# Operand sums, leftover products and fetches reordered in the two half-steps of a diffusion trunk

## The chip, the cores and the metric

The kernel runs on one core of one Trainium2 chip. The metric is the device time of one execution in microseconds. The profile counts from the first to the last instruction of one profiled execution (its span); all times of single instructions come from that execution. PE is TensorE, DVE is VectorE, ACT is ScalarE, POOL is GpSimd, SP is SyncE, which issues transfers.

## The reference, cut to what matters

One layer of a trunk with 640 tokens (512 latent, 128 context) of width 1024, all in float32:

```python
def swiglu(h, w1, w3, w2):
    return (jax.nn.silu(h @ w1) * (h @ w3)) @ w2

def layer(x, mods, l, p, ctx):
    hh = rmsnorm(x, g[0]) * (1 + m[1]) + m[0]
    x = x + 0.5 * m[2] * swiglu(hh, p['ffn1_w1'][l], p['ffn1_w3'][l], p['ffn1_w2'][l])
    hh = rmsnorm(x, g[1]) * (1 + m[4]) + m[3]
    y, ctx_out = token_mixer(hh, p, l, ctx)
    x = x + m[5] * y
    hh = rmsnorm(x, g[2]) * (1 + m[7]) + m[6]
    x = x + 0.5 * m[8] * swiglu(hh, p['ffn2_w1'][l], p['ffn2_w3'][l], p['ffn2_w2'][l])
```

The change lies in the two half-steps, the `swiglu` terms before and after the token mixing. Their inner width is 2816. `m` are the nine modulation vectors, a product of the conditioning with a large matrix.

## The kernel before, in words

**Numbers.** Every float32 matrix operand is held as two parts, high and low (value minus high). A product takes three matmuls per block of 128: high with high, high with low, low with high. ScalarE makes the high part by a copy, VectorE the low part by a subtraction.

**Seven products instead of eight.** The tokens are two halves of 320 columns, the contraction is two halves, and the weights' output columns are two halves. A granule of weights (128 partitions x 2048, 1 MB) is multiplied in Winograd's form of Strassen's scheme: seven products A11, S1, S2, A12, S3, S4, A22 with sums of operand quarters, where the plain form has eight. One product on a granule is 12 matmuls of 128 x 320 (four blocks, three each). They go into three accumulators X, Y, Z; results are finished by additions.

- `operand_sums` makes the four sums S1, S2, S3, S4 of the quarters of the normalised input, each in two halves r: `terms` (a VectorE subtraction or addition in place, in the memory of x, then ScalarE's copy of the high part) and `low` (VectorE). Their VectorE instructions are chained by hand. S4 lies in a quarter of `hm`, S1 to S3 in tiles `S`.
- `Granule.parts` makes from the raw weights the high and low parts of three quarters (`wB`, `wC`) and then forms three sums in place in `raw` (three VectorE instructions). `Granule.sums` splits `raw` as a whole into `ww` high (L286, ScalarE) and low (VectorE). S1, S2, S3 and A22 read `ww`.
- `products` runs over the granules. For granule i TensorE does A11, S1, then A22 of granule i - 1 (`tail[0]`), S2, then S4 of granule i - 1 (`tail[1]`), A12 and S3: so two products of each granule are left over to the next. Beside them stand the load of granule i + 2 into one of two `raw` buffers, `parts` and `sums` of granule i + 1, the copies `u2`, `u3` of accumulators (ScalarE) and the additions that finish results (`done`).

**Stages of a half-step.** Block 0 (256 of the 2816 columns) is done plainly. Then come 20 granules of the up product, w1 and w3 in turn for blocks 1 to 10; the gated results go by `store_g` to `g_dram`. Then the down product reads them back as operands (`fetch`). In the first half-step (`run_whole`) the down product is plain, in three block groups of four granules j each; its weights are split by `Whole.split` (L304), and columns of the modulation are computed beside it on VectorE (L712, from rows `csil` that are read back from `csil_dram`), tied behind `self.at_vec`. In the second half-step (`run`) the down product is plain for the first three blocks and in seven products for two groups of four blocks; there the operand tiles `at[q]` of a later group are fetched into tiles that earlier products have left.

**What sets the order.** TensorE's instructions are kept as written. On the other engines a planner draws the order when the program is built, by a timeline of its own; `tc.issue_after(ins)` adds that the instructions issued under it, on the engine of `ins`, come behind `ins`. Each engine takes its instructions strictly in the drawn order, and so do the queues: `nc.sync` issues on SP, `nc.gpsimd` on POOL. Before the change, in the second half-step, the parts of granule i + 1 are issued behind `copied` (ScalarE's copy of X into Y) and behind `gr.low` (VectorE's part of `sums` of granule i).

Of the kernel before, what the change touches and what calls it, by code (L numbers as in the profile page):

```python
# [31 lines left out]
def tile_trunk(ctx: ExitStack, tc: tile.TileContext, a: dict):  # L32
# [210 lines left out]
    class Granule:  # L243
# [5 lines left out]
        def load(self):  # L249
            self.raw = rawp.tile([128, 2048], F32, tag="raw", name="raw")[:, : 512 * self.nk].rearrange("p (k n) -> p k n", n=256)  # L250
            return self.fetch(self.raw)

# [3 lines left out]
        def parts(self, fp, ties=()):  # L256
            ties = iter(ties)

            def tied(*args):
                with ExitStack() as st:  # L260
                    t = next(ties, None)
                    if t is not None:
                        st.enter_context(tc.issue_after(t.ins))
                    tt(vec, *args)

# [16 lines left out]
        def sums(self):  # L282
            nk = self.nk
            t = self.two(wp, "w", 2048, None)
            flat = self.raw.rearrange("p k n -> p (k n)")
            act(t[0], flat, AF.Copy)  # L286
            self.low = tt(vec, t[1], flat, t[0].bitcast(F32), ALU.subtract)
            for i, o in ((S1, 0), (S3, 128), (A22, 256 * nk), (S2, 256 * nk + 128)):
                self.w[i] = [[w[:, o + 256 * k : o + 256 * k + 128] for k in range(nk)] for w in t]

    class Whole(Granule):


        def split(self, fp=None):
# [8 lines left out]
            for (c0, c1, h), (_, _, lw) in zip(*t):  # L303
                act(h, flat[:, c0:c1], AF.Copy)  # L304
                tt(vec, lw, flat[:, c0:c1], h.bitcast(F32), ALU.subtract)
            self.t = t
# [7 lines left out]
    class HalfStep:  # L314
# [34 lines left out]
        def operand_sums(self, pair):  # L349
# [30 lines left out]
            for f, i, r in (  # L380
                (terms, S1, 0), (terms, S1, 1), (terms, S3, 0), (low, S1, 0), (terms, S2, 0), (low, S1, 1), (terms, S3, 1),
                (terms, S2, 1), (low, S2, 0), (low, S2, 1), (low, S3, 0), (low, S3, 1), (terms, S4, 0), (terms, S4, 1),
            ):
                f(i, r)
                if (f, i) == (low, S2):
                    behind = prev.ins
            low(S4, 0)
            low(S4, 1)
            return behind

# [34 lines left out]
        def products(self, work, between, then=(), behind=None, prepared=False, first=()):  # L425
# [11 lines left out]
            for i, (gr, A, done, used) in enumerate(work):  # L437
# [25 lines left out]
                if self.n_plain < FB and i:  # L463
                    next_parts(copied, gr.low)
                into(Z, S1, True)
                if last:
                    p5 = copy_of(Z, *(("nrv",) if then else ("nt", 2)))
                if tail:
                    tail[0]()
# [4 lines left out]
                into(Y, S2, False)  # L474
                u2 = copy_of(Y, "nacc" if i < 2 * FB - 2 else "nsq", 2)
                if tail:
                    tail[1]()
                into(X, A12, False)
                done(0, 0, X, None)
                between(i, 1)  # L480
                into(Y, S3, False)
                u3 = copy_of(Y, "nry")
                if last:
# [60 lines left out]
        def run_whole(self, x, gate, final, between, behind, first):  # L544
# [6 lines left out]

            def fetch(q, i):
                b0, b1 = PLAIN_GROUPS[q]
                nc.gpsimd.dma_start(out=at[q][i][:, :, : b1 - b0].bitcast(F32), in_=self.g_dram[i, :, :, b0:b1, :])

            order = {A11: (0, 0), S1: (0, 1), S2: (0, 2), A12: (0, 3), S4: (1, 0), A22: (1, 1), S3: (1, 2)}
            work[-1][3] = lambda i: fetch(*order[i])
            self.products(work, between, down[:2], behind=behind, first=first)
# [18 lines left out]
            for q in G:  # L577
                last = q == G[-1]
                for j in range(4):
                    m = 4 * q + j  # L580
                    if m + 2 < len(down):
                        down[m + 2].load()
                    if m + 1 < len(down):
                        down[m + 1].split(self.fp if last and j < 2 else None)
                    for hf in range(1 if last and j else 2):
                        between(len(work) + m, hf)
                        for f in range(2):
                            unit(q, j, f, hf)
# [6 lines left out]

        def run(self, x, gate, final, behind=None, first_ties=()):

# [17 lines left out]

            def between(i, at):
                if (i, at) == (0, 1):
                    with tc.issue_after(work[1][0].low.ins):
# [6 lines left out]
            def down_done(q, j):  # L625
# [8 lines left out]
                def used(i):  # L634
                    if (q, j, i) == (1, 1, S3):
                        fetch(2, A11, nc.gpsimd)
                        fetch(2, S1, nc.gpsimd)
                    elif q == 1 and j == 3 and i in moves:
# [90 lines left out]
    with ExitStack() as ph:  # L729
# [133 lines left out]
        hs.gate_plain(1, 1, ps)  # L863
        hs.operand_sums(lambda r: x_all[:, 2 * r : 2 * r + 2, :])
        x_stack.close()
# [1159 lines left out]
    for f in range(2):  # L2025
        hs.gate_plain(f, 1, (ps[f, 0], ps[f, 1]))
    summed = hs.operand_sums(lambda r: x_pairs[r])
    for g in range(4):
        nc.sync.dma_start(out=x_pairs[g], in_=x2_dram[:, 2 * g : 2 * g + 2, :])
    hs.run(  # L2030
        lambda: x, half_m[:, 1], lambda d, hf: nc.sync.dma_start(out=a["y"][:, d, half(hf)], in_=x[d][:, half(hf)]),
        behind=summed, first_ties=[normed_last] * 5,
    )
# [128 lines left out]
```

## Time and profile before

| | |
|---|---|
| median of 3 runs | 1828.14 us (1828.11 to 1829.18) |
| profiled execution | 1830.94 us, span 1829.2 us |
| granted TensorE clock, mean | 0.993 |
| TensorE (PE) busy | 1788.6 us, 98% |
| VectorE (DVE) busy | 1293.0 us, 71% |
| ScalarE (ACT) busy | 830.3 us, 45% |
| chain that ended last | PE 88%, DVE 5%, DMA 4%, ACT 2% |

A row of the timeline gives the start in the span, the duration, the engine, the source line, the operation with output and inputs, the count of instructions merged into the row, and in brackets how long the engine was idle before and what released it. The line is that of a helper: L39 is any two-operand VectorE instruction, L52 any matmul, so the tiles' names tell instructions apart. A row of the waits gives who waited for whom, the sum in us, the count, and the longest. A row of windows gives the stretch, its length, busy time and count of PE, weight loads, DVE, ACT and POOL, the granted clock, the busy share of the transfer engines and GB/s. A row of a transfer queue gives packets, MB and share of the 16 engines: q0 is POOL's queue, q1 is SP's. A row of a transfer gives the count, KB of each, and the median time from issue to landing.

### The profile page before, as it was taken

How to read it: one execution, taken by the hardware profiler on the slowest of the kernel's cores; microseconds unless marked ns; L12 is line 12 of the kernel's file. 1: busy time of each engine (PE TensorE's matmuls, PEld its weight loads, DVE VectorE, ACT ScalarE, POOL GpSimd, SP SyncE). 2: the span in 40 equal slices, each digit the busy share in tenths (PEclk: the TensorE clock that was granted, in tenths of full speed). 3: DMA queues.
4: the chain of work that ended last, by engine and by line, in shares of the span. 5: the costliest groups of instructions: out<-in, count | busy, mean ns of one | idle time of the engine just before them, and what ended most of it. 6: DMA issues, size and time to landing. Idle time of an engine off the chain costs nothing.

```text
span 1829.2 us, 30479 instructions
## 1 busy us (share of the span) xinstructions
PE 1788.6 (98%) x12498; PEld 1757.0 (96%) x12498; DVE 1293.0 (71%) x2188; ACT 830.3 (45%) x1439; POOL 51.6 (3%) x93
## 2 busy tenths in 40 slices
PE   6999999999999999999999999999999899999989
PEld 4999999999999999999999999899999899999989
DVE  6888886485776668665665458787768778886576
ACT  6644544112654453444544465562326445553232
POOL 0000001010000000000000000000000000000000
PEclk9999999999999999999999999999999999999999
DMA  8344438963334234232232355676542445557952
GB/s 336 121 173 155 159 136 315 350 223 109 127 110 139 85 121 146 75 119 77 75 111 92 104 169 158 212 248 213 198 179 72 156 150 188 175 182 275 343 211 83
DMA packets 127244, 304.98 MB, mean 167 GB/s; under 512 B 9985, under 2 KB 89217, under 8 KB 114433
## 3 DMA queue, kind: packets, MB, share of 16 engines
q1 hardware_dynamic: 116242, 257.09, 40.9%
q0 software_dynamic: 10864, 45.95, 7.4%
q8 instruction: 98, 1.61, 0.4%
q14 instruction: 40, 0.33, 0.1%
HBM read 234.20 MB, written 63.63 MB: 163 GB/s over the span
## 4 chain that ended last, share of the span: by engine, by line
PE 88%; DVE 5%; DMA 4%; ACT 2%; issue 1%; SPq 0%; DVEq 0%; ACTq 0%
PE ps_f L52 44%; PE ps_p L52 22%; PE ps_t L52 11%; PE sc L52 2%; PE ps_o L52 2%; PE ps_n L52 2%; DMA ada<-csil_dram 2%; PE ps_u L52 1%; PE ps_wT L55 1%; DVE junk L712 1%; DVE wL L39 1%; DMA raw_a<-in_w_ada_c 1%; DMA raw_a<-in_w_ada_k 1%; DMA x<-in_x 1%; DMA zT_dram<-so 0%
## 5 line engine op out<-in xcount | busy, mean ns | idle before, releaser
L52 PE MATMUL ps_f<-S,ww 128*128 128x320 f32 x1992 | 319.9, 310 | 5.6 <-ACT ww L286 3.8
L52 PEld LDWEIGHTS ps_f<-S,ww 128*128 128x128 f32 x1992 | 300.6, 189 | 6.1 <-ACT ww L286 4.1
L52 PE MATMUL ps_p<-hH,wH 128*128 128x320 f32 x864 | 273.4, 316 | 0.0
L52 PE MATMUL ps_p<-hH,wL 128*128 128x320 f32 x864 | 267.0, 309 | 0.0
L52 PE MATMUL ps_p<-hL,wH 128*128 128x320 f32 x864 | 266.8, 309 | 0.0
L52 PE MATMUL ps_f<-hm,ww 128*128 128x320 f32 x1248 | 200.5, 313 | 7.7 <-ACT ww L286 4.1
L52 PEld LDWEIGHTS ps_f<-hm,ww 128*128 128x128 f32 x1248 | 189.9, 191 | 8.7 <-ACT ww L286 4.4
L52 PE MATMUL ps_t<-wH,hH 128*128 128x256 f32 x640 | 184.5, 288 | 2.2 <-DVE qT L39 1.7
L52 PE MATMUL ps_t<-wH,hL 128*128 128x256 f32 x640 | 181.3, 283 | 1.1 <-DVE hL L39 1.1
L52 PE MATMUL ps_t<-wL,hH 128*128 128x256 f32 x640 | 180.9, 283 | 0.0
L39 DVE TENSOR_TENSOR ww<-raw,ww 128x2048 fp32r<-128x2048 f32 (+1 forms) x62 | 138.8, 2238 | 41.3 <-ACT ww L286 27.0
L52 PEld LDWEIGHTS ps_p<-hL,wH 128*128 128x128 f32 x864 | 162.5, 188 | 0.5
L52 PEld LDWEIGHTS ps_p<-hH,wH 128*128 128x128 f32 x864 | 162.4, 188 | 0.5
L52 PEld LDWEIGHTS ps_p<-hH,wL 128*128 128x128 f32 x864 | 162.2, 188 | 0.0
L52 PE MATMUL ps_f<-hm,wB 128*128 128x320 f32 x1008 | 161.5, 309 | 0.0
L52 PEld LDWEIGHTS ps_f<-hm,wB 128*128 128x128 f32 x1008 | 151.3, 188 | 0.0
L39 DVE TENSOR_TENSOR wL<-raw,wH 128x2048 fp32r<-128x2048 f32 x49 | 112.1, 2289 | 40.4 <-ACT wH L122 40.3
L122 ACT ACTIVATE wH<-raw 128x2048 fp32r<-128x2048 f32 x49 | 93.7, 1912 | 75.1 <-PE ps_p L52 70.4
L52 PEld LDWEIGHTS ps_t<-wH,hH 128*128 128x128 f32 x640 | 122.6, 192 | 3.1 <-PE ps_t L52 2.3
L39 DVE TENSOR_TENSOR raw<-raw 128x1024 f32<-128x1024 f32 x144 | 124.5, 865 | 1.4
L52 PEld LDWEIGHTS ps_t<-wH,hL 128*128 128x128 f32 x640 | 122.5, 191 | 1.5 <-DVE hL L39 1.5
L52 PEld LDWEIGHTS ps_t<-wL,hH 128*128 128x128 f32 x640 | 122.6, 192 | 0.2
(295 smaller groups left out, 3156.9 us busy)
## 6 DMA issues: line engine op xcount, KB each, us to landing
g_dram<-g SPq DMA_DIRECT2D x44, 640.0 KB, 4.2
raw_a<-in_w_ada_c SPq DMA_DIRECT2D x32, 512.0 KB, 3.9
raw<-in_w1b SPq DMA_DIRECT2D x11, 1024.0 KB, 4.8
raw<-in_w3b SPq DMA_DIRECT2D x11, 1024.0 KB, 6.7
raw<-in_w1a SPq DMA_DIRECT2D x10, 1024.0 KB, 4.9
raw<-in_w3a SPq DMA_DIRECT2D x10, 1024.0 KB, 4.8
hm<-g_dram POOLq DMA_DIRECT2D x8, 1280.0 KB, 10.1
raw_a<-in_w_ada_k SPq DMA_DIRECT2D x8, 1024.0 KB, 11.2
```

Source lines behind the costliest of these rows:

```text
L39: return eng.tensor_tensor(out=out, in0=in0, in1=in1, op=op)
L52: tc.keep_in_program_order(nc.tensor.matmul(*args, **kw))
L55: tc.keep_in_program_order(nc.tensor.transpose(*args, **kw))
L122: act(h, raw, AF.Copy)
L712: vec.tensor_tensor_reduce(out=junk, in0=raw, in1=self.csil[:, v, :], op0=ALU.mult, op1=ALU.add, scale=1.0, scalar=0.0, accum_out=mod[:, c ...
```

## The change

Four things are done.

- `operand_sums` no longer makes S4 at its end; it returns a function `last` that does, and the point `behind` which the next parts follow is now the end of S3's low parts. In the second half-step `rest` calls it from `between(0, 0)`, tied behind the last VectorE instruction of granule 1's parts, and issues the four reloads of x behind it. In the first half-step it is called at once, as before.
- In the up product of the second half-step, for granules 1 and 2, the leftover product A22 goes ahead of S1 instead of behind it.
- There, and in the second half-step's down products, the additions and copies of `tail[1]`, of A12 and `u3` are tied behind the next granule's last in-place sum (VectorE) and behind its high part of `ww` (ScalarE); and a granule's parts are tied behind the high part of the `sums` before.
- Fetches: in the first half-step the three tiles S4, A22 and S3 of block group 1 are fetched on SP behind the weight loads of the first three granules of the down product, instead of on POOL at the end of the up product; and the modulation is tied behind the low part of the weights' split. In the second half-step the first two tiles of group 2 are fetched on SP behind the load of group 1's last granule, instead of on POOL.

```diff
@@ -248,7 +248,8 @@

         def load(self):
             self.raw = rawp.tile([128, 2048], F32, tag="raw", name="raw")[:, : 512 * self.nk].rearrange("p (k n) -> p k n", n=256)
-            return self.fetch(self.raw)
+            self.loaded = self.fetch(self.raw)
+            return self.loaded

         def two(self, pool, tag, n, bufs):
             return [pool.tile([128, n], F32R, tag=tag + c, name="w" + tag, bufs=bufs)[:, : n // 4 * self.nk] for c in "HL"]
@@ -261,7 +262,7 @@
                     t = next(ties, None)
                     if t is not None:
                         st.enter_context(tc.issue_after(t.ins))
-                    tt(vec, *args)
+                    self.at_vec = tt(vec, *args)

             nk, raw = self.nk, self.raw
             lo, hi = raw[:, :, 0:128], raw[:, :, 128:256]
@@ -283,7 +284,7 @@
             nk = self.nk
             t = self.two(wp, "w", 2048, None)
             flat = self.raw.rearrange("p k n -> p (k n)")
-            act(t[0], flat, AF.Copy)
+            self.high = act(t[0], flat, AF.Copy)
             self.low = tt(vec, t[1], flat, t[0].bitcast(F32), ALU.subtract)
             for i, o in ((S1, 0), (S3, 128), (A22, 256 * nk), (S2, 256 * nk + 128)):
                 self.w[i] = [[w[:, o + 256 * k : o + 256 * k + 128] for k in range(nk)] for w in t]
@@ -302,7 +303,7 @@
                 t = [((0, 1024, B[i]), (1024, n, C[i])) for i in range(2)]
             for (c0, c1, h), (_, _, lw) in zip(*t):
                 act(h, flat[:, c0:c1], AF.Copy)
-                tt(vec, lw, flat[:, c0:c1], h.bitcast(F32), ALU.subtract)
+                self.low = tt(vec, lw, flat[:, c0:c1], h.bitcast(F32), ALU.subtract)
             self.t = t

         def w(self, i, k, f):
@@ -379,14 +380,19 @@

             for f, i, r in (
                 (terms, S1, 0), (terms, S1, 1), (terms, S3, 0), (low, S1, 0), (terms, S2, 0), (low, S1, 1), (terms, S3, 1),
-                (terms, S2, 1), (low, S2, 0), (low, S2, 1), (low, S3, 0), (low, S3, 1), (terms, S4, 0), (terms, S4, 1),
+                (terms, S2, 1), (low, S2, 0), (low, S2, 1), (low, S3, 0), (low, S3, 1),
             ):
                 f(i, r)
-                if (f, i) == (low, S2):
-                    behind = prev.ins
-            low(S4, 0)
-            low(S4, 1)
-            return behind
+            behind = prev.ins
+
+            def last(ins=None):
+                nonlocal prev
+                prev = ins or prev
+                for f in (terms, low):
+                    for r in range(2):
+                        f(S4, r)
+
+            return behind, last

         def store_g(self, SO, b):

@@ -461,11 +467,14 @@
                 into(X, A11, True)
                 copied = act(Y, X, AF.Copy)
                 if self.n_plain < FB and i:
-                    next_parts(copied, gr.low)
+                    next_parts(copied, gr.low, gr.high)
+                early = tail and self.n_plain < FB and i in (1, 2) and not prepared
+                if early:
+                    tail[0]()
                 into(Z, S1, True)
                 if last:
                     p5 = copy_of(Z, *(("nrv",) if then else ("nt", 2)))
-                if tail:
+                if tail and not early:
                     tail[0]()
                 if not last:
                     work[i + 1][0].sums()
@@ -473,13 +482,23 @@
                     then[0].split()
                 into(Y, S2, False)
                 u2 = copy_of(Y, "nacc" if i < 2 * FB - 2 else "nsq", 2)
+                def behind_parts():
+                    st = ExitStack()
+                    if self.n_plain < FB and (i in (1, 2) or prepared) and not last:
+                        for t in (work[i + 1][0].at_vec, work[i + 1][0].high):
+                            st.enter_context(tc.issue_after(t.ins))
+                    return st
+
                 if tail:
-                    tail[1]()
+                    with behind_parts():
+                        tail[1]()
                 into(X, A12, False)
-                done(0, 0, X, None)
+                with behind_parts():
+                    done(0, 0, X, None)
                 between(i, 1)
                 into(Y, S3, False)
-                u3 = copy_of(Y, "nry")
+                with behind_parts():
+                    u3 = copy_of(Y, "nry")
                 if last:
                     done(1, 1, p5, u3)
                     into(Z, S4, False)
@@ -549,12 +568,12 @@
             G = range(len(PLAIN_GROUPS))
             at = [[self.ops[i] for i in (A11, S1, S2, A12)], [self.ops[i] for i in (S4, A22, S3)], [self.ops[i] for i in (S1, S2)]]

-            def fetch(q, i):
+            def fetch(q, i, eng=nc.gpsimd):
                 b0, b1 = PLAIN_GROUPS[q]
-                nc.gpsimd.dma_start(out=at[q][i][:, :, : b1 - b0].bitcast(F32), in_=self.g_dram[i, :, :, b0:b1, :])
+                eng.dma_start(out=at[q][i][:, :, : b1 - b0].bitcast(F32), in_=self.g_dram[i, :, :, b0:b1, :])

             order = {A11: (0, 0), S1: (0, 1), S2: (0, 2), A12: (0, 3), S4: (1, 0), A22: (1, 1), S3: (1, 2)}
-            work[-1][3] = lambda i: fetch(*order[i])
+            work[-1][3] = lambda i: order[i][0] == 0 and fetch(*order[i])
             self.products(work, between, down[:2], behind=behind, first=first)
             for q, tag, nb in ((1, "gA", 4), (2, "SO", 4), (2, "gB", 3)):
                 at[q].append(self.fp.tile([128, 2, nb, HALF], F32R, tag=tag, name="op"))
@@ -579,9 +598,13 @@
                 for j in range(4):
                     m = 4 * q + j
                     if m + 2 < len(down):
-                        down[m + 2].load()
+                        loaded = down[m + 2].load()
+                    if m < 3:
+                        with tc.issue_after(loaded):
+                            fetch(1, m, nc.sync)
                     if m + 1 < len(down):
                         down[m + 1].split(self.fp if last and j < 2 else None)
+                        self.at_vec = down[m + 1].low
                     for hf in range(1 if last and j else 2):
                         between(len(work) + m, hf)
                         for f in range(2):
@@ -593,7 +616,7 @@
                 for f in range(2):
                     unit(G[-1], j, f, 1)

-        def run(self, x, gate, final, behind=None, first_ties=()):
+        def run(self, x, gate, final, behind=None, first_ties=(), rest=None):


             def nothing(*args):
@@ -614,6 +637,8 @@
             first = self.SO

             def between(i, at):
+                if (i, at) == (0, 0):
+                    rest(work[1][0].at_vec)
                 if (i, at) == (0, 1):
                     with tc.issue_after(work[1][0].low.ins):
                         self.store_g(first, 0)
@@ -633,8 +658,9 @@

                 def used(i):
                     if (q, j, i) == (1, 1, S3):
-                        fetch(2, A11, nc.gpsimd)
-                        fetch(2, S1, nc.gpsimd)
+                        with tc.issue_after(last[3][0].loaded):
+                            fetch(2, A11)
+                            fetch(2, S1)
                     elif q == 1 and j == 3 and i in moves:
                         fetch(2, moves[i], nc.gpsimd)

@@ -861,7 +887,7 @@
             for k in range(KT):
                 hs.plain(ps[i], W[i], 1, 1, k)
         hs.gate_plain(1, 1, ps)
-        hs.operand_sums(lambda r: x_all[:, 2 * r : 2 * r + 2, :])
+        hs.operand_sums(lambda r: x_all[:, 2 * r : 2 * r + 2, :])[1]()
         x_stack.close()
         hs.store_g(hs.SO, 0)

@@ -2024,12 +2050,16 @@
                 hs.plain(ps[f, i], W[i], f, 1, k)
     for f in range(2):
         hs.gate_plain(f, 1, (ps[f, 0], ps[f, 1]))
-    summed = hs.operand_sums(lambda r: x_pairs[r])
-    for g in range(4):
-        nc.sync.dma_start(out=x_pairs[g], in_=x2_dram[:, 2 * g : 2 * g + 2, :])
+    summed, fourth = hs.operand_sums(lambda r: x_pairs[r])
+
+    def rest(ins):
+        fourth(ins)
+        for g in range(4):
+            nc.sync.dma_start(out=x_pairs[g], in_=x2_dram[:, 2 * g : 2 * g + 2, :])
+
     hs.run(
         lambda: x, half_m[:, 1], lambda d, hf: nc.sync.dma_start(out=a["y"][:, d, half(hf)], in_=x[d][:, half(hf)]),
-        behind=summed, first_ties=[normed_last] * 5,
+        behind=summed, first_ties=[normed_last] * 5, rest=rest,
     )


```

## The prediction

> **What bounds the kernel now.** I read the page first, then TensorE's waits, then the timeline around the long ones, then windows with the granted clock, then the transfers.
>
> ```profile
> span 1829.2 us, 30479 instructions
> PE 1788.6 (98%) x12498; PEld 1757.0 (96%) x12498; DVE 1293.0 (71%) x2188; ACT 830.3 (45%) x1439; POOL 51.6 (3%) x93
> PE ps_f L52 <- ACT ww L286: 8.0, 2, 4.1
> PE ps_f L52 <- DVE ww L39: 5.4, 3, 2.2
> ```
>
> TensorE is the bound; only time in which it waits or runs slowly can be won. The `ps_f` rows are 13.4 us, nearly all of it at three places in the half-steps. In the second half-step, `L286` is `sums` of a granule. Its first place, in time order (each product is 12 matmuls):
>
> ```profile
> 1428.72 1.92 PE L52 MATMUL ps_f<-S,ww 128*128 128x320 f32 x12
> 1430.48 1.92 PE L52 MATMUL ps_f<-hm,wB 128*128 128x320 f32 x12
> 1438.58 3.04 PE L52 MATMUL ps_f<-S,ww 128*128 128x320 f32 x10 [1.77 <-DVE ww L39]
> 1444.55 1.92 PE L52 MATMUL ps_f<-S,ww 128*128 128x320 f32 x12
> ```
>
> The pitch of a product is 1430.48 - 1428.72 = 1.76 us, 0.147 a matmul. The product A11 of granule 1 starts at 1430.48; S1, A22 of granule 0 and S2 follow. S2 should start at 1430.48 + 3 x 1.76 = 1435.76 and starts at 1444.55: **8.79 us lost**. The second place (granules of block group 1 of the down product) and the third (first half-step, down product):
>
> ```profile
> 1740.32 1.92 PE L52 MATMUL ps_f<-S,wB 128*128 128x320 f32 x12
> 1755.12 1.92 PE L52 MATMUL ps_f<-S,wC 128*128 128x320 f32 x12
> 340.43 2.21 PE L52 MATMUL ps_f<-hm,ww 128*128 128x320 f32 x14
> 344.81 2.58 PE L52 MATMUL ps_f<-hm,ww 128*128 128x320 f32 x10 [2.16 <-DVE ww L39]
> 349.68 1.92 PE L52 MATMUL ps_f<-hm,ww 128*128 128x320 f32 x12
> 346.00:348.00 2.00, 2.00 (x10) 2.00 (x9) 2.00 (x6) 0.00 (x0) 0.36 (x1) 0.50 0.72 259
> ```
>
> From 1740.32 to 1755.12 run four products, 7.04 us; 14.80 passed: **7.76 lost**. From 340.43 to 349.68 run three, 5.28; 9.25 passed: **3.97 lost** at a wait of 2.16. The last row, a window, says why a wait costs more than itself: behind it the granted clock (third column from the end) is 0.50, where undisturbed windows (such as 1425 to 1430, below) have 1.00. Together 8.79 + 7.76 + 3.97 = 20.5 us can be won.
>
> [...] The third place went to 0.50 after 2.16, so I price leftover waits by that row, 1.8 us on top.
>
> **The change, first place.** Who held `ww` of granule 1:
>
> ```profile
> 1425.04 1.55 DVE L39 TENSOR_TENSOR x<-x 128x640 f32<-128x640 f32 x2
> 1426.51 1.22 DVE L39 TENSOR_TENSOR wB<-raw,wB 128x1024 fp32r<-128x1024 f32 x1
> 1427.65 0.69 DVE L39 TENSOR_TENSOR wC<-raw,wC 128x512 fp32r<-128x512 f32 x1
> 1428.25 1.56 DVE L39 TENSOR_TENSOR hm<-x,hm 128x640 fp32r<-128x640 f32 x2
> 1429.72 1.22 DVE L39 TENSOR_TENSOR raw<-raw 128x1024 f32<-128x1024 f32 x1
> 1431.56 1.41 DVE L39 TENSOR_TENSOR raw<-raw 128x512 f32<-128x512 f32 x2
> 1432.84 1.05 ACT L271 ACTIVATE wB<-raw 128x1024 fp32r<-128x1024 f32 x1
> 1434.30 1.90 ACT L286 ACTIVATE ww<-raw 128x2048 fp32r<-128x2048 f32 x1
> 1436.23 2.29 DVE L39 TENSOR_TENSOR ww<-raw,ww 128x2048 fp32r<-128x2048 f32 x1 [3.26 <-ACT ww L286]
> ```
>
> The fourth operand sum is four VectorE instructions (two `x<-x`, two `hm<-x,hm`), mixed into the five of the next granule's parts. Moved behind them, the parts run from 1425.04: 1.14 + 0.60 (pitches) + 1.22 + 1.41 = 1429.41. The new tie to `gr.high` puts the later granule's ScalarE parts (1432.84 to 1434.30) behind this `ww`; the copy runs 1429.41 + 1.90 = 1431.31, VectorE's low part ends at 1431.33 + 2.29 = 1433.62, against 1438.52 now. The leftover product A22 goes ahead of S1, so S1 starts at 1430.48 + 3.52 = 1434.00 and needs the low part with its third matmul, 1434.29: covered by 0.67 us. What is late next: A22 needs ScalarE's copy `u3`, ready at 1430.68 but queued on ScalarE behind `ww` and perhaps behind the two copies of the moved sum:
>
> ```profile
> 1427.50 0.73 ACT L373 ACTIVATE hm<-x 128x640 fp32r<-128x640 f32 x1
> 1430.68 0.44 ACT L422 ACTIVATE u<-ps_f 128x320 f32<-128x320 f32 x1 [1.32 <-PE ps_f L52]
> ```
>
> Directly behind `ww` it ends at 1431.75, before A22's 1432.24; behind both copies at 1431.31 + 1.46 + 0.44 = 1433.21, 0.97 late. I take the middle, 0.5. The other end: both copies and both low parts of the moved sum get ahead of `ww`; then its low part ends at 1433.62 + 1.46 + 1.47 = 1436.55, a wait of 2.26, with the clock 4.1 left over. Below nothing is excluded: product order is fixed, and TensorE does no less.
>
> The moved sum itself: its product S4 comes at 1434.00 + 3.52 = 1437.52, its low parts follow `ww` on VectorE and end at 1433.62 + 1.47 = 1435.1: nothing. Granule 2: parts from about 1436.9 (an addition 0.4 and the store's subtraction 1.4 come first), then 4.37, 1.90 and 2.29 end at 1445.5; its S1, again one product later, needs it at 1446.6. Covered by 1.1. The same rows give the early A22 nothing where `ww` is on time: it only swaps two products.
>
> The four reloads of x go with the sum to about 1435.1 on SP, ahead of or behind the load of granule 3:
>
> ```profile
> x<-x_dram SPq DMA_DIRECT2D x4, 640.0 KB, 5.3
> raw<-in_w3b SPq DMA_DIRECT2D x9, 1024.0 KB, 6.9
> 1425.00:1430.00 5.00, 5.00 (x36) 5.00 (x35) 5.00 (x8) 2.24 (x4) 0.00 (x0) 1.00 1.00 326
> ```
>
> That load could issue at 1433.6 after the change, when granule 1's buffer is free. Behind all of x (4 x 640 KB = 2.62 MB, 8.0 us at 326 GB/s) and its own 1.05 MB (3.2) it lands at 1446.3; ScalarE wants it at 1445.5, and 1.05, 4.37, 1.90 and 2.29 from there end at 1455.9, against 1457.2 needed (granule 3's S1 is not early: 12.32 - 1.76 behind granule 2's). Nothing, with 1.3 to spare.
>
> **Second place.** Two group-2 fetches go from POOL to SP, behind the last load of group 1:
>
> ```profile
> 1718.35 0.70 POOL L610 DMA_DIRECT2D S<-g_dram  x1 [3.25 <-PE ps_f L52]
> hm<-g_dram POOLq DMA_DIRECT2D x4, 1280.0 KB, 7.5
> 1720.39 0.97 SPq L74 DMA_DIRECT2D raw<-in_w2b  x2
> q0 software_dynamic: 133, 0.68, 82.4%
> q1 hardware_dynamic: 133, 0.14, 19.1%
> 1735.24 0.44 ACT L422 ACTIVATE u<-ps_f 128x320 f32<-128x320 f32 x1 [4.86 <-PE ps_f L52]
> 1735.58 1.05 ACT L271 ACTIVATE wB<-raw 128x1024 fp32r<-128x1024 f32 x1
> ```
>
> The weights of granule 2 are issued at 1720.39 into fetches of 1280 KB each, of which the first of the two is the row of 1718.35. From 1726 to 1728 both queues get 133 packets, but POOL's (q0) carry 0.68 MB and the weights' (q1) 0.14. ScalarE starts the parts at 1735.58, so the weights were there by then. Two fetches less (2.62 MB at 0.34 MB/us) is 7.7 us less beside them: there by 1727.9, ahead of granule 1's A11 (1740.32 - 7 x 1.76 = 1728.00), behind which and one copy ScalarE takes them, at 1730.4. Then 1.05, VectorE's 4.37 with one residual between (put at 0.7, half the 1.41 row), 1.90 and 2.29 end at 1740.7; S1 needs it at 1742.08 + 0.29 = 1742.37. Covered by 1.7, since the additions tied behind the parts no longer hold them. The bound: ScalarE keeps the parts behind `u` (1735.24). Then 1735.68 + 1.05 + 4.37 + 1.90 + 2.29 = 1745.3, a wait of 2.9, with the clock 4.7 left over. The two fetches are read at group 2's start, three granules of 12.32 us behind 1728.00. The copy `u3` and the evictions tied behind the parts release nothing that TensorE reaches before the next granule's S1, which needs those parts itself: nothing.
>
> **Third place.** Three of the seven fetches at the end of the up product go from POOL to SP, behind the weights.
>
> ```profile
> raw<-in_w2a SPq DMA_DIRECT2D x2, 512.0 KB, 27.1
> q0 software_dynamic: 349, 1.71, 82.0%
> q1 hardware_dynamic: 346, 0.39, 21.4%
> 308.80 28.68 DMA ada<-csil_dram
> 342.47 2.28 DVE L39 TENSOR_TENSOR ww<-raw,ww 128x2048 fp32r<-128x2048 f32 x1
> ```
>
> The weights took 27.1 us, `csil` 28.68 beside POOL's fetches (315 to 320: 349 packets against 346). VectorE then ran three modulation products and split `ww` at 342.47, just as TensorE wanted it. With three fetches (3.9 MB) less on POOL at about 0.34 MB/us both land some 12 us sooner, near 323 and 326. The split's buffer is free when TensorE leaves the granule before last, 340.43 - 7 x 1.76 = 328.1; a copy of about 1.9 and VectorE's 2.28 end at 332, ten before the need: 3.97 won. The new at_vec keeps modulation behind the split: nothing. On SP the first waits until TensorE has left S4; a weight load then stands behind at most one fetch, 1.31 MB or some 4 us at the 0.34, and each granule of the down product lasts 8 x 1.76 = 14 us; group 1 is read only four granules on.
>
> **The sum:** 20.5 - 0.5 = 20.0 us. The profiled execution took 1830.94, its span 1829.2; the span should be 1809.2, that execution 1810.9. The median shown, 1828.14, is 2.80 below it; from it I forecast 1808.1.
>
> **Rivals.** (1) The moved sum gets ahead of `ww`: 4.1 left at the first place, 1828.1 - 16.4 = 1811.7. For it: the order on ScalarE today shows parts ahead of `ww`. Against: the low parts need copies that come after it. Chance 0.14. (2) ScalarE keeps granule 2 behind `u`: 1828.1 - 20.0 + 4.7 = 1812.8; 0.08. (3) Queues change nothing: bytes are the same, so the weights land as late; the third place stays and the second keeps 4.7: 1808.1 + 8.7 = 1816.8. Against it stand the packet rows. [...] 0.10. (4) Slower: granule 3's load waits on SP behind x, and each microsecond past 1446.3 + 1.3 = 1447.6 stalls TensorE. To eat 20 us it must land at 1467.6, 2.62 + 1.05 MB from 1435.1 at 113 GB/s where the window shows 326. 0.03. (5) It does not do what it says: the drawn order stays and the time too; 0.04, since the ties are between instructions of one engine and hold. All three places closed: 0.61.
>
> **How the numbers follow.** Cases 1 to 3 reach 1816.8; with them 0.93. The range is 1805.5 (leftover nothing, other small waits 2 us shorter) to 1817.3. No change is within 0.2%, 3.7 us, what a measurement of this kernel can tell. Faster 0.93, same 0.04, slower 0.03.
>
> **What would show it.** TensorE's waits without the two `L286` rows; the clock 1.00 where it is 0.50 now; `hm<-x,hm` of the fourth sum behind the raw subtractions; loads of `raw` near 5 us where 27.1 stands. Wrong would be: a new `ps_f` wait on `u`, on `S`-operands, or on weights behind x.

## The result, and the profile after

| | before | after |
|---|---|---|
| median | 1828.66 us (1828.11 to 1830.55, 4 runs) | 1810.57 us (1807.82 to 1811.79, 4 runs) |
| profiled execution | 1830.94 us, span 1829.2 us | 1811.79 us, span 1810.0 us |

The ratio is 0.9897, 95% interval 0.988 to 0.9914: 18.8 us less (15.7 to 21.9). First two lines of the page of the changed kernel, then its waits of TensorE on `ps_f`, both of them:

```profile
span 1810.0 us, 30471 instructions
PE 1782.4 (98%) x12498; PEld 1751.8 (97%) x12498; DVE 1293.9 (71%) x2188; ACT 831.0 (46%) x1439; POOL 48.2 (3%) x88
```

```profile
PE ps_f L52 <- DVE hm L39: 2.7, 2, 1.5
PE ps_f L52 <- ACT u L428: 0.4, 1, 0.4
```

The 13.4 us of waits on `ww` (8.0 and 5.4 before) are gone altogether. One wait is new, 0.4 on a copy `u`. The timeline of TensorE at the three places, first, second, third:

```profile
1427.67 1.92 PE L52 MATMUL ps_f<-hm,wB 128*128 128x320 f32 x12
...
1431.19 3.68 PE L52 MATMUL ps_f<-S,ww 128*128 128x320 f32 x24
...
1443.51 2.65 PE L52 MATMUL ps_f<-S,ww 128*128 128x320 f32 x17
...
1728.68 1.92 PE L52 MATMUL ps_f<-S,wB 128*128 128x320 f32 x12
1730.44 5.44 PE L52 MATMUL ps_f<-hm,ww 128*128 128x320 f32 x36
1735.72 1.92 PE L52 MATMUL ps_f<-S,wC 128*128 128x320 f32 x12
...
341.82 3.68 PE L52 MATMUL ps_f<-hm,ww 128*128 128x320 f32 x24
345.34 1.92 PE L52 MATMUL ps_f<-S,ww 128*128 128x320 f32 x12
```

Each place is on pitch (1.76 us a product): 1443.51 - 1427.67 = 15.84 is nine products, 1735.72 - 1728.68 = 7.04 four, 345.34 - 341.82 = 3.52 two. From here on, what a place *loses* is the time between the starts of two products there, less 1.76 for each product between them. Before, the places lost 8.79, 7.76 and 3.97, together 20.5; now nothing.

The span fell by 19.2. Of the other 1.3 us, 1.1 went at the start, where the kernels do not differ. The product `S,ww` of the row 91.12 (in the timeline of before: 90.51) is 0.61 late; the one behind it, 93.40 against 92.27, 1.13. Rows of the stretch from 20 to 60, first before, then after (the granted clock is the third column from the end), and of after's wait:

```profile
20.00:60.00 40.00, 35.06 (x276) 29.70 (x269) 30.04 (x68) 25.36 (x51) 0.00 (x0) 0.91 0.54 221
```

```profile
20.00:60.00 40.00, 35.17 (x276) 29.70 (x277) 29.80 (x70) 25.20 (x50) 0.00 (x0) 0.87 0.54 221
```

```profile
93.40 1.88 PE L52 MATMUL ps_f<-hm,ww 128*128 128x320 f32 x11 [0.36 <-ACT u L428]
```

The twelve kernels below share that start; their clock from 20 to 60 is 0.87 in four and 0.96 in eight, and the wait near 93 is nothing in `f_sum_only`, 0.19 us in `e6_fetch_only` and 1.19 in `u3_third`. `e6_fetch_only` and `e8_late_pool`, which lose nothing at any of the three places, stand 2.97 us apart at the same product of the third place (339.51 and 342.48) and 2.87 in their times. So the start alone makes single executions differ by some 3 us. That is why the experiments are read by what a place loses inside its own trace, and times only where a kernel was timed several times.

### The profile page after: what moved, and what is told of

It is laid out like the page before. It is cut to its first block, busy times and chain, and to the rows that moved or that the text cites. A ratio compares the mean times of both kernels' runs of the same rounds, so it can differ in the third digit from the quotient of the medians.

```text
span 1810.0 us, 30471 instructions
## 1 busy us (share of the span) xinstructions
PE 1782.4 (98%) x12498; PEld 1751.8 (97%) x12498; DVE 1293.9 (71%) x2188; ACT 831.0 (46%) x1439; POOL 48.2 (3%) x88
## 4 chain that ended last, share of the span: by engine, by line
PE 90%; DVE 5%; DMA 3%; ACT 1%; issue 0%; SPq 0%; DVEq 0%; ACTq 0%
PE ps_f L52 46%; PE ps_p L52 22%; PE ps_t L52 11%; PE sc L52 2%; PE ps_o L52 2%; PE ps_n L52 2%; PE ps_u L52 1%; PE ps_wT L55 1%; DVE junk L738 1%; DVE wL L39 1%; DMA raw_a<-in_w_ada_c 1%; DMA raw_a<-in_w_ada_k 1%; DMA x<-in_x 1%; DMA zT_dram<-so 0%; DMA csil<-in_c_rows 0%
## 5 line engine op out<-in xcount | busy, mean ns | idle before, releaser
L52 PE MATMUL ps_f<-hm,ww 128*128 128x320 f32 x1248 | 196.1, 309 | 0.4 <-ACT u L428 0.4
L52 PEld LDWEIGHTS ps_f<-hm,ww 128*128 128x128 f32 x1248 | 186.2, 188 | 0.8 <-ACT u L428 0.6
```

The source lines that it names most:

```text
L52: tc.keep_in_program_order(nc.tensor.matmul(*args, **kw))
```

## The experiments

My theory: the three places are independent, and each is closed by one thing that comes earlier: the first by the moved sum, with the early A22 for the last microsecond, the second by the two fetches on SP, the third by the three fetches on SP. The rivals: the places share their gain; or the ties do the work and the queues and the moved sum nothing.

### Each place undone as a whole

`u1_first`, the first place:

```diff
-                early = tail and self.n_plain < FB and i in (1, 2) and not prepared
+                early = None
-                    next_parts(copied, gr.low, gr.high)
+                    next_parts(copied, gr.low)
-                    if self.n_plain < FB and (i in (1, 2) or prepared) and not last:
+                    if self.n_plain < FB and prepared and not last:
     summed, fourth = hs.operand_sums(lambda r: x_pairs[r])
+    fourth()
-        fourth(ins)
```

(with `behind` set in `operand_sums` where it was before; the reloads of x stay where the change put them, here and in `e2_sum_at_once`)

> The first place undone: the fourth sum is made at once, A22 stands behind S1 again, no ties to the high part or behind the next parts. My theory: the three places add, and this one holds 8.79 us. Against the changed kernel 8.8 us are lost between granule 1's A11 and its S2, in the two waits of before (on ScalarE's and on VectorE's part of ww, some 3.9 and 1.8 us) and the slow clock behind them; the down product keeps its gain, and the time is about 1810.6 + 8.8 = 1819.4. Rival: the places share their gain, since a late stage hands its lateness to the next one (a granule that is late gives the transfers more time). Then the second place is at least a few us better off here and the total is under 1816.

`u2_second`, the second place:

```diff
-                    if self.n_plain < FB and (i in (1, 2) or prepared) and not last:
+                    if self.n_plain < FB and i in (1, 2) and not prepared and not last:
-                        with tc.issue_after(last[3][0].loaded):
-                            fetch(2, A11)
-                            fetch(2, S1)
+                        fetch(2, A11, nc.gpsimd)
+                        fetch(2, S1, nc.gpsimd)
```

> The second place undone: the two fetches of group 2 go on POOL's queue again and nothing is tied behind the next granule's parts in the down products. My theory: 7.8 us more, 1818.3, with ScalarE's copy u ahead of the parts of granule 2 and two waits on its ww, some 4 and 3 us. Rival (the places share their gain): under 1816, since granule 1's stage now comes earlier against the same loads or later, and more than 1 us of the 7.8 is missing or added at another place.

`u3_third`, the third place:

```diff
-            work[-1][3] = lambda i: order[i][0] == 0 and fetch(*order[i])
+            work[-1][3] = lambda i: fetch(*order[i])
-                    if m < 3:
-                        with tc.issue_after(loaded):
-                            fetch(1, m, nc.sync)
-                        self.at_vec = down[m + 1].low
```

> The third place undone: all seven fetches on POOL's queue at the end of the up product, the modulation not tied behind the split. My theory: 3.8 to 4.0 us more, 1814.5, in one wait of about 2.2 us on VectorE's ww and a granted clock near 0.50 in the next 4 us; raw<-in_w2a and csil take 27 to 29 us again where they take some 17. Rival: the wait returns without the slow clock, and only 2.2 us are lost.

Measured beside the kernel before (1828.29 us, 7 runs): `u1_first` 1817.03 (ratio 0.9939, 0.9924 to 0.9954), `u2_second` 1818.25 (0.9948, 0.9933 to 0.9963), `u3_third` 1813.72 (0.9916, 0.99 to 0.9933). TensorE's rows of the three kernels, in this order:

```profile
1424.91 1.92 PE L52 MATMUL ps_f<-hm,wB 128*128 128x320 f32 x12
1430.68 0.90 PE L52 MATMUL ps_f<-S,ww 128*128 128x320 f32 x2 [3.85 <-ACT ww L287]
...
1438.19 1.92 PE L52 MATMUL ps_f<-S,ww 128*128 128x320 f32 x12
```

```profile
1725.89 1.92 PE L52 MATMUL ps_f<-S,wB 128*128 128x320 f32 x12
1731.94 0.90 PE L52 MATMUL ps_f<-hm,ww 128*128 128x320 f32 x2 [4.13 <-ACT ww L287]
...
1740.70 1.92 PE L52 MATMUL ps_f<-S,wC 128*128 128x320 f32 x12
```

```profile
340.23 2.22 PE L52 MATMUL ps_f<-hm,ww 128*128 128x320 f32 x14
344.39 2.60 PE L52 MATMUL ps_f<-hm,ww 128*128 128x320 f32 x10 [1.95 <-DVE ww L39]
...
349.25 1.92 PE L52 MATMUL ps_f<-hm,ww 128*128 128x320 f32 x12
```

They lose 13.28 - 5.28 = 8.00, 14.81 - 7.04 = 7.77 and 9.02 - 5.28 = 3.74, each at its own place and nothing at the two others. So the places are independent: the rival of a shared gain falls, and so does "2.2 us without the slow clock" for the third: in `u3_third` the clock is 0.50 from 345 to 348. The 8.00 against 8.79 is no sharing: the wait on ScalarE is 3.85 in both kernels, and the slow clock begins inside it in `u1_first` (0.64 from 1430 to 1431) and behind it before (0.82 from 1437 to 1438; last section). By time, `u2_second` wins 9.5 us over before (6.8 to 12.2), less than the 12.8 of its two closed places (8.79 + 3.97). Its traced execution, 1817.22, is the fastest of its four; no trace shows where the others lost more, and it stays open.

### What closes the first place

`e1_no_early`:

```diff
-                early = tail and self.n_plain < FB and i in (1, 2) and not prepared
+                early = None
```

> Only the early A22 undone: for granules 1 and 2 the product S1 stands ahead of the leftover A22. In the changed kernel A11 of granule 1 starts at 1427.67 and VectorE's part of ww ends at 1430.91 (1428.62 + 2.29); S1 would start at 1429.43 and need it with its third matmul, 1429.72: a wait of about 1.2 us. Theory A (a wait this long already lowers the clock, as 2.16 did in the third place of before): 2 to 3 us lost between A11 and S2. [...] Theory C (the early A22 is not needed): 0. For granule 2 ww's low part ends at 1442.85 against S1 one product earlier, 1441.75 + 0.29: some 0.8 us by the same sums.

`e2_sum_at_once`:

```diff
     summed, fourth = hs.operand_sums(lambda r: x_pairs[r])
+    fourth()
-        fourth(ins)
```

> Only the fourth sum is made at once again, ahead of granule 1's parts; the early A22 and the ties stay. My theory: the four VectorE instructions of the sum, mixed into the parts, make ww late. From the changed kernel's rows (raw subtractions end at 1426.5, ww's high part 1426.67 to 1428.6) plus the 4 times 0.77 us of the sum, ww's high part ends near 1431.9 and its low part near 1434.2, where S1 needs it at 1431.5: a wait of 2.7 us, with the slower clock 4.5 lost. Rival: the ties alone had put the parts in order and moving the sum did nothing: 0 lost.

`e3_no_up_ties`:

```diff
-                    next_parts(copied, gr.low, gr.high)
+                    next_parts(copied, gr.low)
-                    if self.n_plain < FB and (i in (1, 2) or prepared) and not last:
+                    if self.n_plain < FB and prepared and not last:
```

> In the up product of the second half-step no ties: neither the next parts behind the high part of ww, nor the additions and copies behind the next parts. The moved sum and the early A22 stay. My theory: granule 1 needs none of them (its sum is moved, and the order of its parts is as in the changed kernel); granule 2 gets the store's subtraction and the additions between its parts, its low part of ww ends near 1444.8 where S1 needs it at 1443.8: a wait of 1 us. So 1 us is lost if a short wait costs only itself, 2 to 3 if the clock falls. Rival: the ties carry the first place, and more than 4 us are lost at granule 1.

`f_sum_only` is `e1_no_early` and `e3_no_up_ties` together, run after them:

> The first place with the moved sum alone: no early A22 for granules 1 and 2, no ties in the up product. Theory A (the sum carries it, the two others add the small waits that they cost alone): 1.3 us lost at granule 1, as with the early A22 alone undone, and 0 to 1.5 at granule 2, where two additions stand between the parts and S1 comes one product sooner, but 1.3 us of delay have been given: 1.3 to 2.9 together of the 8.0 that go with all undone. Theory B (the early A22 and the ties are what makes the moved sum work): over 4.4, as much as with the sum alone undone.

One execution of each was timed: `e1_no_early` took 1811.36 us, `e2_sum_at_once` 1814.15, `e3_no_up_ties` 1811.39, `f_sum_only` 1811.51. Timelines of the first three, and a window with the clock behind the waits for the first two:

```profile
1425.92 1.92 PE L52 MATMUL ps_f<-hm,wB 128*128 128x320 f32 x12
...
1429.21 1.73 PE L52 MATMUL ps_f<-S,ww 128*128 128x320 f32 x10 [1.07 <-DVE ww L39]
...
1432.54 1.92 PE L52 MATMUL ps_f<-S,ww 128*128 128x320 f32 x12
```

```profile
1430.00:1432.00 2.00, 2.00 (x16) 2.00 (x15) 2.00 (x4) 0.70 (x2) 0.00 (x0) 1.00 0.98 393
```

```profile
1425.34 1.92 PE L52 MATMUL ps_f<-hm,wB 128*128 128x320 f32 x12
...
1429.83 0.55 PE L52 MATMUL ps_f<-S,ww 128*128 128x320 f32 x2 [0.80 <-ACT ww L287]
1432.15 3.49 PE L52 MATMUL ps_f<-S,ww 128*128 128x320 f32 x22 [1.77 <-DVE ww L39]
1435.48 1.92 PE L52 MATMUL ps_f<-hm,wC 128*128 128x320 f32 x12
...
1437.92 1.91 ACT L287 ACTIVATE ww<-raw 128x2048 fp32r<-128x2048 f32 x1 [6.36 <-DVE raw L39]
1439.74 0.42 ACT L428 ACTIVATE u<-ps_f 128x320 f32<-128x320 f32 x1
1440.21 2.02 PE L52 MATMUL ps_f<-S,ww 128*128 128x320 f32 x12 [1.05 <-ACT u L428]
```

```profile
1432.00:1434.00 2.00, 1.85 (x12) 1.85 (x13) 2.00 (x3) 0.00 (x0) 0.00 (x0) 1.00 0.40 70
```

```profile
1443.35 3.49 PE L52 MATMUL ps_f<-S,ww 128*128 128x320 f32 x22 [0.90 <-DVE ww L39]
```

- `e1_no_early` loses 6.62 - 5.28 = 1.34, with the clock at 1.00 behind the wait of 1.07: neither the 2 to 3 us of theory A nor theory C's 0. The early A22 is needed, for 1.3 us. For granule 2 nothing is lost (0.8 was expected): the delay at granule 1 gives its parts that much more time.
- `e2_sum_at_once` loses 4.4, as I had written, but not as I had worked it out. Granule 1 loses 10.14 - 7.04 = 3.1 in two waits with the clock at 1.00 throughout. The other 1.3 are a wait that I had not seen. On ScalarE granule 2's `ww` stands ahead of the copy `u2` and waits 6.36 us for VectorE's late sums in `raw`; `u2` comes at 1439.74, and TensorE needs the accumulator that it empties. This is not shown to be the work of a tie: `u2` is not among the copies that the ties hold back, and `u1_first`, without these ties, has the same order (`ww` at 1438.78, `u` at 1440.59). There it costs nothing, since TensorE comes to S2 only at 1438.19.
- `e3_no_up_ties` loses nothing at granule 1 and 1.17 at granule 2 (S1 starts at 1441.99, the product two behind it at 1446.68, 3.52 would be pitch), as expected. The ties are worth that much here.
- `f_sum_only` loses 1.34 at granule 1 (A11 at 1425.87, S2 at 1432.49) and 0.21 at granule 2, 1.55 of the 8.00 that go with all undone. Theory A: the moved sum alone (with the new point `behind`) closes some 6.4 of them, and the early A22 and the ties share the rest.

### What closes the second place

`e4_queue_only` drops the ties in the down products (the first line pair of `u2_second`), `e5_ties_only` puts the fetches back on POOL (its second).

> In the down products of the second half-step no additions or copies are tied behind the next parts; the two fetches stay on SP behind the weights. My theory: the weights' earlier landing puts the parts ahead of the copy u by itself, so this is within 0.5 us of the changed kernel at the second place. Rival: the ties carry the second place; then some 4 us or more are lost there (the copy u ahead of granule 2's parts on ScalarE, as before).

> The counterpart: the two fetches of group 2 are on POOL's queue again, the ties in the down products stay. My theory: the weights come late and the copy u is drawn ahead of granule 2's parts; the ties keep the additions behind them, so ww's low part is late by about 2.9 us, some 4.7 with the slower clock, where 7.8 go with both undone. Rival (ties carry it): 0 to 1 us lost. Rival (queue alone carries it): the whole 7.8.

One execution of each took 1812.1 and 1816.5 us. Timelines, `e4_queue_only` first:

```profile
1780.23 1.73 PE L52 MATMUL ps_f<-hm,ww 128*128 128x320 f32 x10 [0.94 <-DVE ww L39]
```

```profile
1725.98 1.92 PE L52 MATMUL ps_f<-S,wB 128*128 128x320 f32 x12
1727.94 0.42 ACT L468 ACTIVATE ps_f<-ps_f 128x320 f32<-128x320 f32 x1 [5.14 <-PE ps_f L52]
1728.28 1.90 ACT L287 ACTIVATE ww<-raw 128x2048 fp32r<-128x2048 f32 x1
1730.23 0.56 PE L52 MATMUL ps_f<-hm,ww 128*128 128x320 f32 x2 [2.32 <-ACT ww L287]
...
1739.99 1.92 PE L52 MATMUL ps_f<-S,wC 128*128 128x320 f32 x12
```

`e4_queue_only` loses nothing at the second place, so the moved fetches close it without these ties. The tie of a granule's parts to the high part of the `sums` before stays in this kernel; `e3_no_up_ties` lacks it, has the others there, and loses nothing at this place either. No run drops all of them. What `e4_queue_only` loses, 1.20 (S1 starts at 1778.83, the next product at 1781.79), is at a later granule, where additions stand between the parts again; that I had not foreseen. At the second place `e5_ties_only` loses 14.01 - 7.04 = 6.97, not the 4.7 that I had put: nine tenths of `u2_second`'s 7.77. My sum let ScalarE begin `ww` when VectorE's sums in `raw` were done; but with the parts late, `L468`, the same granule's copy of X into Y, stands ahead of it and waits for TensorE's A11 to end (1725.98 + 1.92 = 1727.90). So ScalarE, which had missed its slot, was held 5.14 us by the next thing in its order, not only by its own lateness.

What made the parts late seems to be the drawn order more than the landing of the weights. In the kernel before, with the same fetches on POOL, SP's queue moved 0.99 MB from 1723 to 1731, nearly all of granule 2's weights of 1.05 MB, and the parts began at 1735.58. In `e5_ties_only` ScalarE began on them at 1721.24, behind `u` (1720.90), for which it had waited 4.86 us for TensorE. So much of what the fetches on POOL cost seems to come from the place that the planner gave the parts, and less from the transfer itself; no run moves the fetches and keeps the order.

### What closes the third place

`e6_fetch_only` drops the tie of the modulation (the last line of `u3_third`), `e7_tie_only` puts the fetches back on POOL at the end of the up product (its other lines). `e8_late_pool` issues the three fetches on POOL too, but later:

```diff
-                    if m < 3:
-                        with tc.issue_after(loaded):
-                            fetch(1, m, nc.sync)
+                    if m == 2:
+                        with tc.issue_after(self.col.ins):
+                            [fetch(1, k) for k in range(3)]
```

(`self.col` is POOL's latest load of modulation columns.)

> First half-step: the three fetches go on SP behind the weights, the modulation is not tied behind the split. My theory: the fetches do it, since the weights and csil both land some 10 us sooner: 0 lost against the changed kernel at the third place, at most 0.5. Rival: without the tie the modulation products stand ahead of the split, and more than 2 us are lost.

> First half-step: the tie stays, but all seven fetches are on POOL's queue at the end of the up product. My theory: raw<-in_w2a lands after some 27 us again, and the wait of about 2 us with its slow clock comes back: 3.8 to 4 us lost. Rival: the tie puts the split ahead of the modulation, which alone is 5 us of VectorE's time, and 0 to 1 us are lost.

> The three fetches of the first half-step are issued on POOL's queue after all, but only after the up product, tied behind a later load of POOL's, once the third weight load of the down product has been issued. Theory A (it is the transfers that compete at the time of the first weights, not the queue as such): 0 to 0.5 us lost against the changed kernel; raw<-in_w2a of the first granules takes some 17 us as there. Theory B (anything on POOL's queue beside SP's slows SP's loads by its share of packets, and the first ones are still under way): the wait of 2 us comes back, 3.8 lost. A later wait on a weight load, for granule 4 or 5, would be a third way.

One execution of each took 1809.85, 1812.6 and 1812.72 us. `e7_tie_only` loses 3.76 (product starts 338.55 and 347.59, three apart), like `u3_third`'s 3.74; the tie alone does nothing. Its wait:

```profile
342.72 1.92 PE L52 MATMUL ps_f<-hm,ww 128*128 128x320 f32 x10 [1.95 <-DVE ww L39]
```

`e6_fetch_only` and `e8_late_pool` lose nothing and have no wait of TensorE from 330 to 350. So the queue as such is not it: POOL's queue does as well when the fetches start late (the first two at 343.74, with the weights of this place landed). The rows of VectorE that say what was late, of the changed kernel and of `u3_third`:

```profile
329.09 1.23 DVE L738 CUSTOM_DVE_ANT_0 ada<-ada 128x1024 bf16<-128x1024 f32 x1 [5.05 <-DMA ada<-csil_dram]
...
333.94 2.28 DVE L39 TENSOR_TENSOR ww<-raw,ww 128x2048 fp32r<-128x2048 f32 x1
```

```profile
337.20 1.23 DVE L738 CUSTOM_DVE_ANT_0 ada<-ada 128x1024 bf16<-128x1024 f32 x1 [13.82 <-DMA ada<-csil_dram]
...
342.06 2.28 DVE L39 TENSOR_TENSOR ww<-raw,ww 128x2048 fp32r<-128x2048 f32 x1
```

The split stands some 5 us behind the landing of `csil` with the tie and without it. What moved is that landing, 8 us (in `e8_late_pool` VectorE gets `csil` at 329.74); the tie never put the split ahead of it.

## Why the prediction was right, point by point

**The sum.** 20.0 of 20.5 us were to be won at three places; 20.5 were won. The start took 1.1 back in the profiled execution (1811.79 against the forecast 1810.9). The median, 1810.57 against 1808.1, is further off, for I took the distance of median to profiled execution, 2.80, over from before; it is 1.2 after. That distance differs from execution to execution, and it should have stood in the forecast as an uncertainty of 2 us, not as a term.

**First place.** The order came out as worked: the moved sum behind the parts, `ww` directly behind them.

```profile
1426.67 1.92 ACT L287 ACTIVATE ww<-raw 128x2048 fp32r<-128x2048 f32 x1
1428.49 0.42 ACT L428 ACTIVATE u<-ps_f 128x320 f32<-128x320 f32 x1
1428.62 2.29 DVE L39 TENSOR_TENSOR ww<-raw,ww 128x2048 fp32r<-128x2048 f32 x1 [0.52 <-ACT ww L287]
1428.81 1.36 ACT L374 ACTIVATE hm<-x 128x640 fp32r<-128x640 f32 x2
```

The low part ends at 1430.91, 0.57 ahead of S1's third matmul (1431.19 + 0.29); 0.67 was forecast. The one step that failed here is the 0.5 left over for `u3`: it went directly behind `ww` (1428.49) and ahead of the copies of the moved sum, and A22 started on pitch. I took the middle of two orders where only one could come. By `e2_sum_at_once`, the nearest run, rival 1's price of 4.1 would have been about right, but by luck: it held 1.8 for a slow clock that did not come there, and lacked the 1.3 of the wait on `u`.

**Second place.** ScalarE took the parts of granule 2 one A11 earlier, ahead of `u`, as forecast, and rival 2 did not come.

```profile
1718.65 1.05 ACT L272 ACTIVATE wB<-raw 128x1024 fp32r<-128x1024 f32 x1
...
1723.60 0.44 ACT L428 ACTIVATE u<-ps_f 128x320 f32<-128x320 f32 x1 [3.38 <-PE ps_f L52]
...
1727.59 2.28 DVE L39 TENSOR_TENSOR ww<-raw,ww 128x2048 fp32r<-128x2048 f32 x1
```

The cover was 1730.44 + 0.29 - 1729.87 = 0.86, where 1.7 was forecast: I had said that the additions no longer hold the parts, but three of them stand on VectorE between `ww`'s high and low part (from 1725.36 on), and the low part began 0.68 after the high part had ended (1726.91). For the kernel before, the forecast had the weights come too late for the parts to go ahead of `u`, and read their landing from the start of the parts (1735.58). That was only a bound: in the kernel before SP's queue had moved 0.99 of the granule's 1.05 MB from 1723 to 1731, and the parts then stood behind `u` by the drawn order. So the order was forecast rightly, the lateness of the weights too large. Rival 2's price of 4.7 was too low, as `e5_ties_only` shows (6.97).

**Third place.** 3.97 won, by fewer fetches beside `csil` and the weights. Sizes were off, without effect: the weights that had taken 27.1 us took 17.7, where I had named near 5 as the sign, and `csil` was there 19.1 us after its issue (310.03 to 329.09) instead of 28.68, 9.6 sooner where I had put 12. The sum also had the split follow the weights at once, with the modulation behind it; but the three modulation products stayed ahead of this split, which ended at 336.22 (333.94 + 2.28) where 332 was forecast, still before TensorE came to its product at 341.82. While POOL's four fetches ran (315 to 320), the queues' shares of the engines were what they had been before, 80.3% for q0 and 22.7% for q1; the fetches were only over sooner.

```profile
raw<-in_w2a SPq DMA_DIRECT2D x2, 512.0 KB, 17.7
```

**Rivals 3 to 5.** Queues did change something (`e4_queue_only`, `e6_fetch_only`). Granule 3's load was not queued behind all of x, since SP's order put it between the reloads: x at 1427.40, `raw` at 1430.94, x at 1433.48. The ties held.

## What to carry to other kernels

Measure what a place loses by the starts of the same products, not by the sum of its waits: 13.4 us of waits stood for 20.5. Look for what must come earlier (a sum in front of the parts, a fetch beside a needed load) before tying orders: here the kernels without ties and early product lose 1.55 (`f_sum_only`), 1.20 (`e4_queue_only`) and nothing (`e6_fetch_only`), so the moved sum and the moved fetches bring about 17.8 of the 20.5 us, if these losses add; no run drops all at once. An order that is right only while its inputs are on time makes a late input worse, as `L468` ahead of `ww` did in `e5_ties_only` (ScalarE idle for 5.14 us) and `ww` ahead of `u` in `e2_sum_at_once` (6.36).

## What was not expected of the hardware

**The clock behind a wait.** Windows of 1 us of the kernel before show where the granted clock goes from 1.00 to 0.50:

```profile
24.00:25.00 1.00, 1.00 (x12) 0.78 (x5) 1.00 (x2) 0.00 (x0) 0.00 (x0) 0.76 1.02 410
345.00:346.00 1.00, 1.00 (x6) 1.00 (x6) 1.00 (x4) 0.00 (x0) 1.00 (x2) 0.69 0.61 137
1437.00:1438.00 1.00, 0.00 (x0) 0.00 (x0) 1.00 (x1) 0.00 (x0) 0.00 (x0) 0.82 0.00 0
```

It is 1.00 again from 28, 349 and 1445 on. At the third place a wait of 2.16 us in the kernel before, and of 1.95 in `u3_third` and in `e7_tie_only`, was followed by 0.50 and lost 3.97, 3.74 and 3.76. The waits of 1.07 in `e1_no_early`, 0.94 in `e4_queue_only` and 0.90 in `e3_no_up_ties` lost only 1.34, 1.20 and 1.17. In `e2_sum_at_once` waits of 0.80, 1.77 and 1.05 were followed by 1.00 up to 1450. So the row that I priced by (any wait near 2 us costs 1.8 more) does not hold for the 1.77 there.

The place of the fall differs too. In the kernel before the clock was still 1.00 from 1436 to 1437, behind the wait of 3.85 that ended at 1436.25, and fell in the next one, of 1.77. In `u1_first` it fell inside the wait of 3.85, which ended at 1430.68 (0.64 from 1430 to 1431). The first place of `u1_first` loses 8.00 where before lost 8.79 for two reasons. Its second wait is 1.42 where before's was 1.77. And more of the slow clock passed while TensorE had nothing to do: about 1.8 us against 0.9 before, an estimate from windows of 1 us with 1.00 and 0.50 as the only two clocks, by which it began near 1430.3 there and near 1437.6 before. At 0.50 that is about 0.45 of the 0.79, beside 0.35 for the shorter wait.

Nor does the length of a wait settle when the clock falls. Early in the kernel before a wait of 1.35 us was followed by 0.50, where 1.77 in `e2_sum_at_once` was not:

```profile
44.00:45.00 1.00, 0.00 (x0) 0.00 (x0) 1.00 (x3) 1.00 (x3) 0.00 (x0) 1.00 0.00 0
45.00:46.00 1.00, 0.80 (x3) 0.81 (x4) 1.00 (x4) 1.00 (x4) 0.00 (x0) 0.50 0.00 0
45.20 2.23 PE L52 MATMUL ps_f<-hm,wH 128*128 128x320 f32 x7 [1.35 <-DVE hm L39]
```

What else counts is not shown and stays open.

**The start.** The clock from 20 to 60 differs from run to run: 0.87 after, 0.91 before, 0.96 in `u1_first` and `e6_fetch_only`. The windows below 1.00 are those from 21 to 29 and from 45 to 50 after, from 24 to 28 and from 45 to 49 before, and only those from 23 to 27 in `e6_fetch_only`. There the product `S,ww` starts at 88.98, 2.14 us ahead of after's 91.12. Why the clock differs is not shown. The first fall alone does not decide it, for that lies at the same place in the kernel before and in `e2_sum_at_once` (0.76 from 24 to 25 in both), with 0.91 from 20 to 60 in the one and 0.96 in the other.
